# A hybrid diffusion trunk layer on Trainium2: setting the order of the DMA queue in the second phase of the first feed-forward block

## The chip, the cores and the metric

The kernel runs on one core of a Trainium2 chip, in one launch. The time of a kernel is the device time of the launch in microseconds, as the median of its runs. The engines of the core are named as the profile names them: PE is TensorE (matmuls), PEld its weight loads, DVE is VectorE, ACT is ScalarE, POOL is GpSimd, and SP is SyncE, which here only issues DMA transfers.

## The reference

One layer of a transformer-like trunk is computed on 1024 latent tokens and 256 context tokens, all of width 1024, in float32:

```python
# m_l, m_c: nine modulation vectors each, from silu(c) @ ada_w + ada_b (latent) and c_ctx (context)
x   = x   + 0.5 * m_l[2] * swiglu(modulate(rms_norm(x,   norm1_w), m_l[0], m_l[1]), ffn1_w1, ffn1_w3, ffn1_w2)
ctx = ctx + 0.5 * m_c[2] * swiglu(modulate(rms_norm(ctx, norm1_w), m_c[0], m_c[1]), ffn1_w1, ffn1_w3, ffn1_w2)
y   = token_mixing(modulate(rms_norm(x, norm2_w), ...), modulate(rms_norm(ctx, norm2_w), ...), ...)
x   = x + m_l[5] * y
x   = x + 0.5 * m_l[8] * swiglu(modulate(rms_norm(x, norm3_w), ...), ffn2_w1, ffn2_w3, ffn2_w2)
return rms_norm(x, final_norm_w)

def swiglu(h, w1, w3, w2):
    return (silu(h @ w1) * (h @ w3)) @ w2
```

The hidden width of the feed-forward blocks (FFN1 and FFN2) is 2816. The change lies in FFN1, in the product with w2 for the latent tokens and in what is done beside it.

## The kernel before

**Precision.** TensorE multiplies in a reduced float32 format. So each operand is split into a high part and a low part (`split`: ScalarE writes the high part, L59; VectorE, for some tiles GpSimd, subtracts it to get the low part, L60), and each product is three matmuls (`mm3`: high x high at L64, high x low at L65, low x high at L66).

**Order.** A scheduler at build time puts the instructions of each engine into a fixed list, which the engine then works off in order, waiting at each instruction for what it needs. It goes through time by its own estimate of durations and takes for each engine the ready instruction of the best priority; a tile is ready to be written when its room is free. The priority is the place in the program; inside `high_priority(offset=n)` it is n places earlier, with a negative n later (`low(n)` gives n places later). Inside `manual_schedule(engines=...)` the instructions of these engines keep the order in which the program lists them.

**FFN1, first phase** (`hidden`, `chain`). The 22 slices of the hidden width are taken in pairs. The latent tokens are two halves of 512 (tg 0 and 1). Of a pair of slices and the two halves, a 2 x 2 block product, seven products are formed instead of eight, from sums of tiles. The inputs of these sums, T1 to T4, stand ready as split tiles. T4 has the room `hh10`, `hl10` to `hh13`, `hl13` (the first half of the room of `self.h[1]`), and is read by the last of the seven products of each chain (`prod(w4, t4, a, False)`). `g_out` writes seven combinations of the gated results of each pair to device memory (`gd[1..7, p]`, p = 0 to 10), and `w2_sums` two combinations of the weights w2 (`sd[0..1, p]`).

**FFN1, second phase** (`back6`, then `prod(4, ...)` later). The product with w2 is formed the same way, six of its seven products in `back6`, in the order 1, 2, 6, 5, 7, 3. Each product has 11 steps (p), and a step is 12 matmuls: one tile of g, one of the weights, four output blocks, `mm3` each. In each step `pair` loads g's raw tile (`raw_half(self.gd[i, p])`, L260), splits it into one of four rooms `h{h,l}00` to `h{h,l}03`, loads the weight tile (`w2_tile`) and splits it into one of six rooms `whi`, `wlo`, all 150 places ahead (`WPRI`). Raw tiles of g and of the weights share six rooms named `raw` (`NR`). For products 7 and 3 the weight is a difference of two loaded tiles, which have eight rooms of their own, `h{h,l}04` to `h{h,l}07` (`raw2`, L368; L392 subtracts).

**Beside the second phase** `feed` runs one entry of `plan` per step. It loads the context tokens (`load_x`, eight tiles of 128 KB, L777) at steps 0 to 7, and the sixteen tiles of x (L1465), which were given up during the first phase, at steps 8, 10, ... 38; and it makes the first norm of the context (`ctx1`, in steps 22, 24, 27 and 30 to 37). All of these are placed by the scheduler like all else, as early as it finds room. After products 2, 7 and 3 the results are added to x (`add4`, L442); later x is written to device memory (`spill`, L1507).

**After it** comes the context's own FFN1 (`classic` and `Y`, pairs of slices). Beside it the second half (tg 1) of the latent tokens gets its second norm: `norm2(1, 0)` sums the squares (L173, L176, L177) ahead of the loop, and one further entry of `pend` is listed behind each pair: entry 1 forms the column sums on TensorE (`rstd_col`, L186) and the root (L1049, L1050), entry 2 spreads it over the rows (`rstd_rows`, L193, L202, and L1477), entries 3 to 10 write one normed tile each into the room of `self.h[1]` (`norm_k`, L216, L217, L222). Then follow `prod(4)`, the context's projections, the mixing stage, FFN2 and the final norm.

Of the kernel before, what the change touches and what calls it, by code (L numbers as in the profile page):

```python
# [2 lines left out]

# [7 lines left out]
F32 = mybir.dt.float32  # L11
# [5 lines left out]
P = 128  # L17
D = 1024
KD = D // P
DFF = 2816  # L20
NF = DFF // P
NP = NF // 2
# [8 lines left out]
class Trunk:  # L31
# [50 lines left out]
    def cond(self):  # L82
        self.cs = [self.cond_row("c")]
        self.junk = self.tile(self.dp, [P, D], mybir.dt.bfloat16, "junk")
        self.ada, self.ab = -1, tuple(range(AB))

# [308 lines left out]
    def hidden(self, f0, mods=lambda: None):  # L395
# [8 lines left out]
        for p in [*range(f0 // 2 - 1), NP - 1]:  # L404
            self.w2_sums(p)

    def pair(self, i, p):
        slots = [f"0{k}" for k in range(4)]
        t = self.hslot(slots[self.nslot % 4])
        self.nslot += 1  # L410
        with self.tc.high_priority(offset=WPRI):
            self.split(self.raw_half(self.gd[i, p]), *t)
            return self.half(self.w2_tile(i, p)), t

    def hslot(self, s):
        return tuple(self.tile(self.hp, [P, 512], F32R, f"h{c}{s}") for c in "hl")
# [107 lines left out]
    def ffn_open(self, i, gates, pool):  # L524
        self.w1, self.w3, self.w2 = (self.I[f"w{i}{j}"] for j in (1, 3, 2))
        self.gates_m, self.fp, self.s, self.g = gates, pool, {}, {}
        self.gd, self.sd = self.gds[i - 1], self.sds[i - 1]
        self.nraw, self.nslot, self.feed = -1, 0, iter(())

    def stile(self):  # L530
        return self.tile(self.fp, [P, 512], F32, "s", self.ns)
# [119 lines left out]
    def first1(self, pools, n1):  # L651
# [52 lines left out]
        for st in range(KD):  # L704
# [6 lines left out]
            if st + 1 < KD:  # L711
                self.mod_col(9 + st, (0,), True)
                if st >= SH:
                    self.mod_col(st + 1, (0,), True)
# [684 lines left out]
    def run(self):  # L1399
        nc, tc, I = self.nc, self.tc, self.I  # L1400
        S = {}

        def opn(name, side="left"):
            S[name] = tc.tile_pool(name=name, bufs=1, reuse_waits="tile", side=side)
            return S[name].__enter__()
# [34 lines left out]
        self.ada, self.ab = -1, (2, 3, 4, 0)  # L1440
        todo = [(8 * m + k, ctxs) for m, ctxs in EMODS for k in range(KD) if m or not 1 <= k <= SH]
        todo.reverse()
# [11 lines left out]
        hc = opn("hc", "right")  # L1454
# [4 lines left out]

        plan = defaultdict(list)  # L1460
        for k in range(KD):
            plan[k].append(lambda k=k: self.load_x((None, None, hc), (2,), (k,)))
        for i, (tg, k) in enumerate((tg, 4 * q + k) for tg, q in ((0, 0), (1, 1), (0, 1), (1, 0)) for k in range(4)):
            o = TGS[tg][0]
            plan[8 + 2 * i].append(lambda tg=tg, k=k, o=o: nc.sync.dma_start(self.x[tg][k], I["xT"][k * P:(k + 1) * P, o:o + 512]))  # L1465
        nrm = {}

        def norm_step(tg, i, a, b):
            n = TGS[tg][1]
            if i == 0:  # L1470
                nrm[tg] = self.squares(self.x[tg], n, n2)
            elif i == 1:
                nrm[tg] = self.rstd_col(nrm[tg], n, n2)
            elif i == 2:
                pr = self.rstd_rows(nrm[tg], n, n2)
                nrm[tg] = self.scr(n2, "nrb")[:, :n]
                nc.scalar.copy(nrm[tg], pr)  # L1477
            else:
                self.norm_k(tg, i - 3, a, b, nrm[tg], n2)

        ctx1 = lambda i: norm_step(2, i, self.mcol(1, 1), self.mcol(0, 1))
        norm2 = lambda tg, i: norm_step(tg, i, self.mcol(4, int(tg == 2)), self.mcol(3, int(tg == 2)))
        for i, at in enumerate((22, 24, 27, *range(30, 30 + KD))):
            plan[at].append(lambda i=i: ctx1(i))

        CT = [(2, 0, 256)]
# [12 lines left out]

        self.feed = feed()  # L1500
        self.psN = self.psB
        self.back6(False)

        def spill(tg):
            o = TGS[tg][0]
# [32 lines left out]
        for tg in LATTG:  # L1538
            o, n = TGS[tg]
# [39 lines left out]

NT2 = 5  # L1580
AB = 5
SH = 2
NR = 6
EMODS = ((5, (0,)), (2, (0, 1)), (1, (1,)), (0, (1,)), (4, (0, 1)), (3, (0, 1)), (7, (0,)), (6, (0,)))
# [39 lines left out]
def layout(inputs):  # L1624
# [7 lines left out]
    A["adaT"] = c(g["ada_w"][0].T).reshape(72, P, D)  # L1632
    A["adaN"] = c(g["ada_w"][0][:, P:(SH + 1) * P].reshape(KD, P, SH, P).transpose(2, 1, 0, 3)).reshape(SH, P, D)
    A["ccol"] = c(np.stack([g["c"].reshape(KD, P), g["c_ctx"].reshape(KD, P)]).transpose(2, 1, 0)).reshape(P, 2 * KD)
# [65 lines left out]
```

## Time and profile before

| | |
|---|---|
| median of 3 runs | 2186.89 us (2180.45 to 2189.05) |
| the profiled execution | 2184.39 us, its span 2182.6 us |
| busy PE, DVE, ACT, POOL | 97%, 70%, 45%, 13% of the span |
| mean granted TensorE clock | 0.993 |
| DMA | 373.39 MB, mean 171 GB/s; 51.9% of 16 engines' span |
| FFN1's second phase (six products) | from 467.3 to 657.5 us |
| the context's FFN1 | from 657.5 us on |

A row of the timeline has the start and the duration in us, the engine, the line of the kernel, the operation with the tiles that it writes and reads, and in brackets the idle time of the engine before it and what ended that. A row of the windows has for each engine the busy time in us and (x) the instructions in that stretch, then the granted clock of TensorE, the mean busy share of the 16 DMA engines and what they moved in GB/s. A matmul that reaches over the edge of a window counts in both. A row of the DMA issues has the number of transfers, the size of one and the median time in us from issue to landing.

### The profile page before, as it was taken

To read this page: it belongs to the slowest core of one execution; us is meant where nothing else is said; L and a number is where in the kernel's file an instruction comes from. 1 tells how busy PE (TensorE), PEld (TensorE's weight loads), DVE (VectorE), ACT (ScalarE), POOL (GpSimd) and SP (SyncE) were. 2 spreads that over 40 slices of the span, in tenths; PEclk is the share of its full clock that TensorE was granted. 3 is DMA by queue.
4 is the path that set the end of the run, shared out by engine and by line. 5 is a ranking of instruction groups with operands and counts; after the bars stand their busy time and mean duration, and the time that the engine had idled before them with its cause. 6 is when DMAs were issued, how large, how long until landed. Compare 5 with 4: busy or idle time off the path is not lost. (4 is left out here: it accounts for less than half of the span.)

```text
span 2182.6 us, 32925 instructions
## 1 busy us (share of the span) xinstructions
PE 2123.4 (97%) x11558; PEld 1807.1 (83%) x11558; DVE 1530.7 (70%) x2735; ACT 981.2 (45%) x1811; POOL 278.1 (13%) x285
## 2 busy tenths in 40 slices
PE   8999999999999999999989999999999999999998
PEld 7888888887789999987777987788878888888888
DVE  7889999755678556744665546758777667664686
ACT  4434334344545545546454335525343433434553
POOL 0000000000016553611132112200000000000000
PEclk8999999999999999999999999999999999999999
DMA  9267768478775566553312322324134444467674
GB/s 330 83 231 245 268 220 276 158 234 278 246 254 179 172 188 197 177 155 104 92 58 70 94 59 90 120 81 166 63 120 158 147 159 159 150 208 249 218 241 145
DMA packets 202934, 373.39 MB, mean 171 GB/s; under 512 B 24016, under 2 KB 37264, under 8 KB 202768
## 3 DMA queue, kind: packets, MB, share of 16 engines
q1 hardware_dynamic: 202336, 371.16, 51.9%
q8 instruction: 90, 1.47, 0.3%
q14 instruction: 76, 0.62, 0.1%
q10 hardware_dynamic: 432, 0.13, 0.0%
HBM read 296.72 MB, written 66.09 MB: 166 GB/s over the span
## 5 line engine op out<-in xcount | busy, mean ns | idle before, releaser
L59 ACT ACTIVATE whi<-raw 128x512 fp32r<-128x512 f32 (+1 forms) x647 | 398.9, 623 | 711.4 <-issue 210.2
L60 DVE TENSOR_TENSOR wlo<-raw,whi 128x512 fp32r<-128x512 f32 (+1 forms) x533 | 368.5, 694 | 307.1 <-ACT whi L59 301.5
L64 PE MATMUL psa<-hh,whi 128*128 128x512 f32 (+1 forms) x1444 | 531.4, 368 | 1.7 <-ACT hh L59 0.7
L65 PE MATMUL psa<-hl,whi 128*128 128x512 f32 (+1 forms) x1444 | 530.9, 368 | 1.0 <-DVE hl L60 1.0
L66 PE MATMUL psa<-hh,wlo 128*128 128x512 f32 (+1 forms) x1444 | 530.0, 367 | 0.0
L64 PEld LDWEIGHTS psa<-hh,whi 128*128 128x128 f32 x1444 | 273.9, 190 | 45.5 <-ACT hh L59 1.4
L65 PEld LDWEIGHTS psa<-hl,whi 128*128 128x128 f32 x1444 | 273.9, 190 | 43.8 <-DVE hl L60 2.5
L66 PEld LDWEIGHTS psa<-hh,wlo 128*128 128x128 f32 x1444 | 273.9, 190 | 41.5
L64 PE MATMUL psb<-hh,whi 128*128 128x512 f32 (+1 forms) x680 | 260.4, 383 | 2.2 <-ACT hh L59 1.7
L65 PE MATMUL psb<-hl,whi 128*128 128x512 f32 (+1 forms) x680 | 260.6, 383 | 1.6 <-DVE hl L60 1.4
L66 PE MATMUL psb<-hh,wlo 128*128 128x512 f32 (+1 forms) x680 | 259.8, 382 | 0.6 <-DVE wlo L60 0.6
L60 POOL TENSOR_TENSOR wlo<-raw,whi 128x512 fp32r<-128x512 f32 (+1 forms) x114 | 153.0, 1361 | 194.3 <-ACT whi L59 188.3
L65 PEld LDWEIGHTS psb<-hl,whi 128*128 128x128 f32 x680 | 127.8, 188 | 29.0 <-DVE hl L60 4.4
L64 PEld LDWEIGHTS psb<-hh,whi 128*128 128x128 f32 x680 | 127.9, 188 | 28.7 <-ACT hh L59 2.8
L66 PEld LDWEIGHTS psb<-hh,wlo 128*128 128x128 f32 x680 | 127.8, 188 | 25.5 <-DVE wlo L60 1.0
L1050 POOL TENSOR_TENSOR nr<-nr,mhalf 128x4 f32<-128x4 f32 (+1 forms) x11 | 11.6, 1057 | 867.7 <-ACT hh L59 482.5
L60 DVE TENSOR_TENSOR hl<-raw,hh 128x512 fp32r<-128x512 f32 x159 | 112.2, 711 | 13.2 <-ACT hh L59 12.2
L59 ACT ACTIVATE hh<-raw 128x512 fp32r<-128x512 f32 x159 | 97.6, 619 | 16.5 <-DMA raw<-gd 14.8
L64 PE MATMUL psa<-whi,hh 128*128 128x256 f32 (+1 forms) x320 | 93.1, 291 | 1.4 <-ACT s L1004 1.2
L65 PE MATMUL psa<-wlo,hh 128*128 128x256 f32 (+1 forms) x320 | 93.4, 292 | 1.0 <-DVE wlo L60 0.9
L66 PE MATMUL psa<-whi,hl 128*128 128x256 f32 (+1 forms) x320 | 92.5, 289 | 0.0
L126 DVE CUSTOM_DVE_ANT_0 junk<-ada,condc,cols 128x1024 bf16<-128x1024 f32 x62 | 79.3, 1279 | 5.4 <-DMA ada<-in_adaT 5.1
(397 smaller groups left out, 3723.2 us busy)
## 6 DMA issues: line engine op xcount, KB each, us to landing
raw<-in_w SPq DMA_DIRECT2D x374, 256.0 KB, 3.0
gd<-s SPq DMA_DIRECT2D x154, 256.0 KB, 2.7
raw<-gd SPq DMA_DIRECT2D x154, 256.0 KB, 3.7
ada<-in_adaT SPq DMA_DIRECT2D x76, 512.0 KB, 4.8
s<-in_w SPq DMA_DIRECT2D x66, 256.0 KB, 4.7
sd<-s SPq DMA_DIRECT2D x44, 256.0 KB, 2.8
hh<-in_w SPq DMA_DIRECT2D x44, 256.0 KB, 3.9
raw<-sd SPq DMA_DIRECT2D x44, 256.0 KB, 3.0
```

The costliest lines, as they stand in the source:

```text
L59: nc.scalar.activation(hi, src, AF.Copy)
L60: (eng or nc.vector).tensor_tensor(out=lo, in0=src, in1=hi.bitcast(F32), op=ALU.subtract)
L64: mm(ps, wa[0], xa[0], start=start, stop=False, skip_group_check=more)
L65: mm(ps, wa[0], xa[1], start=False, stop=False, skip_group_check=more)
L66: mm(ps, wa[1], xa[0], start=False, stop=stop, skip_group_check=more)
L126: nc.vector.tensor_tensor_reduce(out=self.junk, in0=t, in1=self.cs[s], scale=1.0, scalar=self.col("ada_b")[:, j:j + 1], op0=ALU.mult, op1= ...
L1050: nc.gpsimd.tensor_tensor(out=r, in0=r, in1=self.mhalf[:, :n], op=ALU.pow)
```

## The change

Four things are changed, all in the order of work; the arithmetic and the transfers are the same.

1. The loads of g and of the weights in `back6` are no longer issued in the step that uses them, 150 places ahead. `loaded` keeps a list, and lists in each step the loads of the step five later (`AHEAD`), at the priority of its place; the first step lists the loads of the first six. `back6` runs inside `manual_schedule` for SP, so that all the loads listed there, those of `feed` too, keep that order among themselves.
2. The raw tiles of g get rooms of their own: `raw_g` goes round the sixteen rooms `hh10`, `hl10`, `hh11`, ... `hl17` of `self.h[1]`. The six `raw` rooms are left to the weights.
3. The loads in `plan` are spaced otherwise: the context's eight tiles in steps 12, 13, 15, 16, 18, 19, 21 and 22, the tiles of x in the steps of `xat`. The context's norm comes in steps 24, 27, 30 and 33 to 40.
4. Of the second half's norm, entries 1 to 10 are listed 150 places later (`NLOW`).

```diff
@@ -1,4 +1,4 @@
-from collections import defaultdict
+from collections import defaultdict, deque
 from contextlib import ExitStack, nullcontext
 
 import numpy as np
@@ -404,13 +404,32 @@
         for p in [*range(f0 // 2 - 1), NP - 1]:
             self.w2_sums(p)
 
+    def raw_g(self, src):
+        self.ng += 1
+        t = self.tile(self.hp, [P, 512], F32, f"h{'hl'[self.ng % 2]}1{self.ng // 2 % 8}")
+        self.nc.sync.dma_start(t, src)
+        return t
+
+    def loaded(self, i, p):
+        if not self.steps:
+            return self.raw_half(self.gd[i, p]), self.w2_tile(i, p)
+        while len(self.ahead) <= min(AHEAD, self.nsteps):
+            j, q = next(self.steps)
+            self.ahead.append((self.raw_g(self.gd[j, q]), self.w2_tile(j, q)))
+        self.nsteps -= 1
+        return self.ahead.popleft()
+
     def pair(self, i, p):
         slots = [f"0{k}" for k in range(4)]
         t = self.hslot(slots[self.nslot % 4])
         self.nslot += 1
+        if self.steps:
+            g, w = self.loaded(i, p)
         with self.tc.high_priority(offset=WPRI):
-            self.split(self.raw_half(self.gd[i, p]), *t)
-            return self.half(self.w2_tile(i, p)), t
+            if not self.steps:
+                g, w = self.loaded(i, p)
+            self.split(g, *t)
+            return self.half(w), t
 
     def hslot(self, s):
         return tuple(self.tile(self.hp, [P, 512], F32R, f"h{c}{s}") for c in "hl")
@@ -525,7 +544,7 @@
         self.w1, self.w3, self.w2 = (self.I[f"w{i}{j}"] for j in (1, 3, 2))
         self.gates_m, self.fp, self.s, self.g = gates, pool, {}, {}
         self.gd, self.sd = self.gds[i - 1], self.sds[i - 1]
-        self.nraw, self.nslot, self.feed = -1, 0, iter(())
+        self.nraw, self.nslot, self.feed, self.steps = -1, 0, iter(()), None
 
     def stile(self):
         return self.tile(self.fp, [P, 512], F32, "s", self.ns)
@@ -1459,13 +1478,18 @@
 
         plan = defaultdict(list)
         for k in range(KD):
-            plan[k].append(lambda k=k: self.load_x((None, None, hc), (2,), (k,)))
-        for i, (tg, k) in enumerate((tg, 4 * q + k) for tg, q in ((0, 0), (1, 1), (0, 1), (1, 0)) for k in range(4)):
+            plan[12 + k + k // 2].append(lambda k=k: self.load_x((None, None, hc), (2,), (k,)))
+        xat = (1, 4, 7, 10, 24, 26, 28, 30, 32, 34, 36, 38, 39, 40, 42, 43)
+        for at, (tg, k) in zip(xat, ((tg, 4 * q + k) for tg, q in ((0, 0), (1, 1), (0, 1), (1, 0)) for k in range(4))):
             o = TGS[tg][0]
-            plan[8 + 2 * i].append(lambda tg=tg, k=k, o=o: nc.sync.dma_start(self.x[tg][k], I["xT"][k * P:(k + 1) * P, o:o + 512]))
+            plan[at].append(lambda tg=tg, k=k, o=o: nc.sync.dma_start(self.x[tg][k], I["xT"][k * P:(k + 1) * P, o:o + 512]))
         nrm = {}
 
         def norm_step(tg, i, a, b):
+            with self.low(NLOW if tg == 1 and i else None):
+                norm_part(tg, i, a, b)
+
+        def norm_part(tg, i, a, b):
             n = TGS[tg][1]
             if i == 0:
                 nrm[tg] = self.squares(self.x[tg], n, n2)
@@ -1480,7 +1504,7 @@
 
         ctx1 = lambda i: norm_step(2, i, self.mcol(1, 1), self.mcol(0, 1))
         norm2 = lambda tg, i: norm_step(tg, i, self.mcol(4, int(tg == 2)), self.mcol(3, int(tg == 2)))
-        for i, at in enumerate((22, 24, 27, *range(30, 30 + KD))):
+        for i, at in enumerate((24, 27, 30, *range(33, 33 + KD))):
             plan[at].append(lambda i=i: ctx1(i))
 
         CT = [(2, 0, 256)]
@@ -1499,7 +1523,11 @@
 
         self.feed = feed()
         self.psN = self.psB
-        self.back6(False)
+        self.ng, self.ahead, self.nsteps = -1, deque(), 6 * NP - 1
+        self.steps = ((i, p) for i in (1, 2, 6, 5, 7, 3) for p in range(NP))
+        with tc.manual_schedule(engines={mybir.EngineType.SP}):
+            self.back6(False)
+        self.steps = None
 
         def spill(tg):
             o = TGS[tg][0]
@@ -1579,6 +1607,8 @@
 
 NT2 = 5
 AB = 5
+AHEAD = 5
+NLOW = 150
 SH = 2
 NR = 6
 EMODS = ((5, (0,)), (2, (0, 1)), (1, (1,)), (0, (1,)), (4, (0, 1)), (3, (0, 1)), (7, (0,)), (6, (0,)))
```

## The prediction

> **What bounds the kernel now.** I read the page first, then the windows of FFN1's second phase, then the TensorE timeline at its holes, then the DMA views around them.
>
> ```profile
> span 2182.6 us, 32925 instructions
> ## 1 busy us (share of the span) xinstructions
> PE 2123.4 (97%) x11558; PEld 1807.1 (83%) x11558; DVE 1530.7 (70%) x2735; ACT 981.2 (45%) x1811; POOL 278.1 (13%) x285
> ```
>
> TensorE is the bound over the whole span, so only a hole in its stream can be won. The profiled execution took 2184.39 us for this span of 2182.6; the median of the runs, 2186.89, lies 2.5 us above it. The change touches the stretch from 467 to about 720 us. The second phase is six products of eleven steps. One product per row:
>
> ```profile
> core 0: us, PE busy (x) PEld busy (x) DVE busy (x) ACT busy (x) POOL busy (x), PEclk, DMA share, GB/s
> 467.30:497.20 29.90, 29.90 (x134) 24.75 (x133) 18.60 (x32) 10.79 (x20) 0.00 (x0) 1.00 0.88 292
> 497.20:530.90 33.70, 31.30 (x133) 24.52 (x132) 16.35 (x27) 15.66 (x29) 0.00 (x0) 1.00 0.83 266
> 530.90:566.00 35.10, 32.79 (x142) 25.13 (x140) 23.93 (x43) 14.27 (x27) 1.00 (x1) 1.00 0.89 297
> 566.00:597.70 31.70, 31.02 (x134) 24.64 (x134) 20.16 (x36) 19.97 (x39) 0.00 (x0) 1.00 0.68 211
> 597.70:627.60 29.90, 29.90 (x134) 24.75 (x133) 20.75 (x34) 13.17 (x25) 0.00 (x0) 1.00 0.89 297
> 627.60:657.50 29.90, 29.90 (x134) 24.76 (x133) 24.59 (x37) 11.07 (x19) 7.04 (x5) 1.00 0.67 213
> ```
>
> The reader sees that an undisturbed product takes 29.90 us, so a step is 29.90 / 11 = 2.72 us, and that the second to fourth products take 33.70 + 35.10 + 31.70 - 3 x 29.90 = 10.8 us too much. The context norm's eight small matmuls lie in the third; such a group of eight takes 671.92 - 671.01 = 0.9 us (rows further down). **9.9 us of holes** are left. What they wait for:
>
> ```profile
> 522.69 0.39 PE L66 MATMUL psb<-hh,wlo 128*128 128x512 f32 x1
> 524.75 0.50 PE L64 MATMUL psb<-hh,whi 128*128 128x512 f32 x1 [1.68 <-ACT hh L59]
> 525.56 0.50 PE L65 MATMUL psb<-hl,whi 128*128 128x512 f32 x1 [0.30 <-DVE hl L60]
> ```
>
> The split on ScalarE is named, but ScalarE is busy under half of that product; it waits for the tile itself. Meanwhile the queue is full of other transfers:
>
> ```profile
> GB/s 205 275 273 259 303 295 265 325 350 366 169 270 184 271 365 273 129 297 222 284 378 337 222 279 274 249 330 277 305 178 280 285 331 273 357 355 280 270 274 375
> x<-in_xT SPq DMA_DIRECT2D x16, 256.0 KB, 4.7
> hl<-in_w SPq DMA_DIRECT2D x7, 256.0 KB, 4.6
> xd<-x SPq DMA_DIRECT2D x4, 256.0 KB, 5.1
> hh<-in_w SPq DMA_DIRECT2D x2, 256.0 KB, 5.0
> ```
>
> That is the DMA view from 497 to 566 us. All sixteen x tiles and nine weight tiles for products 7 and 3, which start at 566 + 31.7 us, go out here, between the tiles that the next step needs. Only six raw rooms, shared by g and w, give those a lead of three steps.
>
> **The change part by part.** It adds and removes no transfer and no arithmetic: the same 66 g tiles, 66 weight steps, sixteen x and eight context tiles, and the same splits. What moves is order.
>
> *x and context spaced, queue in order.* Four x tiles go out with the first ten steps, eight half-size context tiles with steps 12 to 22, twelve x tiles with steps 24 to 43; the nine early weight tiles go back to their turn. That is 12 + 9 = 21 tiles fewer before step 24, and g and w no longer share six rooms: the rule "next step's tiles first" now holds. Steps 15 to 43 then carry at most 2 + 12/20 = 2.6 tiles per 2.72 us, which even the slowest rate below serves. Each transfer costs its SyncE issue as before. So the 9.9 us go, if nothing takes their place.
>
> *g's raw tiles in h's room.* Something does. Steps 0 to 7 put g into the room of T4, and T4 is what the last product of phase one reads:
>
> ```profile
> 464.54 0.39 PE L64 MATMUL psb<-hh,whi 128*128 128x512 f32 x1
> 464.99 0.39 PE L66 MATMUL psb<-hh,wlo 128*128 128x512 f32 x1
> ...
> 467.26 0.39 PE L64 MATMUL psa<-hh,whi 128*128 128x512 f32 x1
> ```
>
> The first pair of T4 is read until 464.99 + 0.39 = 465.4; g's first tile can't be issued earlier, and as it heads a fixed order, every weight, x and later g tile of the phase is queued behind it on SyncE. Before, these went out from 445 us on:
>
> ```profile
> raw<-gd SPq DMA_DIRECT2D x6, 256.0 KB, 4.6
> raw<-in_w SPq DMA_DIRECT2D x5, 256.0 KB, 4.9
> ```
>
> (DMA view, 440 to 465 us.) These eleven tiles of lead are lost. How long a tile takes to land, and what else the queue has to carry at that time (raw tiles from 440 to 470 us; the window and the issues from 465 to 505 us):
>
> ```profile
> DMA to landing us min/median/max: 2.6/4.2/5.7
> 465.00:505.00 40.00, 40.00 (x178) 33.14 (x177) 25.05 (x42) 16.74 (x34) 0.00 (x0) 1.00 0.85 279
> gd<-s SPq DMA_DIRECT2D x6, 256.0 KB, 3.6
> s<-in_w SPq DMA_DIRECT2D x6, 256.0 KB, 4.7
> sd<-s SPq DMA_DIRECT2D x4, 256.0 KB, 3.7
> ```
>
> First step: g lands at 465.4 + 2.6 = 468.0, w one tile later, its split takes 0.62 (row L59 of the page's groups, shown below). TensorE starts at about 468.0 + 0.85 + 0.62 = 469.5 instead of 467.26: **2.2 us**, or 3.8 with the median landing.
>
> ```profile
> L59 ACT ACTIVATE hh<-raw 128x512 fp32r<-128x512 f32 x159 | 97.6, 619 | 16.5 <-DMA raw<-gd 14.8
> ```
>
> Then the queue must catch up. Step 14, the last before the extra traffic is over, needs 30 tiles for steps 0 to 14, 6 stores of g, 10 transfers of the weight sums and 3 x tiles: 49. With t us per tile it is ready at 465.4 + 2.6 + 48t + 0.62 and wanted at 467.26 + 14 x 2.72 = 505.3. The delay by then, which includes the start, is S = 48t - 36.7, and at least 2.2. The tile time t isn't in the trace for a queue that is never short of requests. Bounds: 0.262 MB at the window's 279 GB/s is 0.94; with its idle share taken out, 0.94 x 0.85 = 0.80. The new queue has up to six weight and sixteen g tiles asked for, so it lies nearer to the second; I take 0.85. S = 4.1 us, with 2.2 to 8.4 for the range. I add 0.8 for short waits of a step whose parts land just in time, like the 0.30 above. **Second phase: 9.9 - 4.1 - 0.8 = 5.0 us gained.**
>
> *Clock.* A gap of over 2 us can cost more than itself. In the context's FFN1, after the phase:
>
> ```profile
> 711.56 0.28 PE L66 MATMUL psb<-ghi,wlo 128*128 128x256 f32 x1
> 713.92 0.38 PE L64 MATMUL psb<-ghi,whi 128*128 128x256 f32 x1 [2.08 <-ACT ghi L59]
> 714.87 0.56 PE L65 MATMUL psb<-glo,whi 128*128 128x256 f32 x1 [0.57 <-DVE glo L60]
> 715.00:718.40 3.40, 3.40 (x16) 3.40 (x17) 3.00 (x4) 0.90 (x2) 2.64 (x2) 0.51 0.53 162
> ```
>
> After two waits close together the granted clock is 0.51 for 3.4 us, which costs 1.7 us; after the gap at 522.69 it stayed 1.00. The start gap of 2.2 us lies between these two cases, so I charge half, **0.8 us lost**. [...]
>
> *Second half's norm at lower priority.* Its column sum on TensorE now stands right behind the first pair of the context's FFN1 and waits for VectorE's nacc:
>
> ```profile
> 671.01 1.05 PE L186 MATMUL psb<-ones,nacc 128*128 128x1 f32 x8 [1.85 <-DVE nacc L177]
> 671.92 0.36 PE L64 MATMUL psa<-hh,whi 128*128 128x256 f32 x1
> 711.30:721.70 10.40, 7.75 (x50) 7.35 (x49) 9.21 (x16) 4.92 (x10) 5.52 (x4) 0.84 0.51 155
> 674.90:680.70 5.80, 5.80 (x50) 5.76 (x49) 5.34 (x9) 2.24 (x5) 4.79 (x4) 1.00 0.42 135
> ```
>
> By the last row 48 matmuls take 5.80 us; a pair of slices has 144, so 17.4 us, and lists some 70 other instructions. 150 places of 214 are about 12 us, by when nacc is long done: **1.9 us gained**. Nobody misses it: the half's normed tiles are first read in the mixing stage. The making of these tiles is another matter. It makes VectorE late at 711 us, where 48 matmuls take 10.40 us: 4.6 us lost, the slow clock among them. They are listed one per pair, behind pairs 3 to 10, and yet run during the first three, in room that the scheduler thought free; a step of 150 doesn't forbid that. They come later and meet other work. Between nothing and 4.6 no row decides; I take half, **2.3 us gained**. The context norm comes two to three steps later and ends at step 40 of 66; it is first used after the phase: nothing.
>
> Sum: 5.0 - 0.8 + 1.9 + 2.3 = 8.4 us. 2184.39 - 8.4 = 2176.0 for a profiled execution; 2.5 more for the median: **2178.5 us**.
>
> **The rivals.** All but the norm's part hangs on t.
>
> *The queue keeps up (t at 0.80 or below).* S is the start alone: 9.9 - 2.2 - 0.8 = 6.9, no clock drop, and the norm's tiles meet nothing: 6.9 + 1.9 + 4.6 = 13.4, so 2173.5. For it: stretches of over 330 GB/s in the view above. Against: nothing here holds them for ten microseconds.
>
> *The hole moves to the front (t about 0.92).* S = 7.5. The last two products take three tiles a step and lose their nine early ones: from step 44 on there are 66 tiles, 4 of x, 4 spills and 6 weights of the context's FFN1 that find the raw rooms free, 80 in all, against 22 x 2.72 = 59.8 us and a lead of three steps (four rooms for the splits of g), 8.2: 80 x 0.92 - 68.0 = 5.6 late. 9.9 - 7.5 - 5.6 + 1.9 = -1.3, so 2188: no change.
>
> *The queue falls behind at both ends (t of 1.0 or more): slower.* The same two terms. The mean over the phase supports it:
>
> ```profile
> DMA packets 26997, 48.92 MB, mean 257 GB/s; under 512 B 2995, under 2 KB 3379, under 8 KB 26983
> ```
>
> (480 to 670 us.) 0.262 MB at 257 GB/s is 1.02. S = 12.3, the end is 80 x 1.02 - 68.0 = 13.6 late, together 25.9 against 9.9 before and 1.9 won: 14.1 slower, 2201. At t = 1.0 it is 11.5; from there it counts as slower. Against it: this mean holds stretches with nothing asked for. For it: a fixed order can hold the queue idle too, as one transfer that waits for its room stops all behind it. [...] That is a rule against a fixed order; the start here shows its price, the 2.2 us, and the trace shows no more of it.
>
> *The lower priority does nothing.* Then 1.9 and 2.3 are missing: 2182.7, inside the forecast's range.
>
> **How the numbers follow.** 0.5%, 10.9 us, is about what a measurement of this kernel can tell from no change. Forecast with its own range of 2175 to 2184: 0.46, a quarter of it beyond 10.9 us. Queue keeps up: 0.27, faster. Hole moves: 0.13, the same. Slower: 0.14. Faster 0.27 + 0.11 = 0.38, same 0.35 + 0.13 = 0.48, slower 0.14. The range goes down to 2170, where all that the sum names is won (9.9 + 1.9 + 4.6 = 16.4), and up to 2193, where t is about 0.96; beyond lie some 0.05 and 0.10.
>
> **What would show it.** Right: g's first load issued at 465 us, a TensorE gap of 2 to 4 us at 467; small holes until about 505, none from 510 to 657; x tiles one to three steps apart; the column sum some 10 us later, without wait; the first product at 32 to 34 us, the next five near 29.9. Wrong: first product still at 29.9 (T4's room doesn't bind); holes after 585 (the end binds); DVE waits in the context's FFN1 as long as before; or changes of several microseconds after 900 us, where the change writes nothing but a new order could come out of the scheduler.

## The result and the profile after

The change made the kernel slower. The median of five runs each went from 2186.89 us (2180.45 to 2189.05) to 2199.86 us (2196.58 to 2201.57); the ratio is 1.0059, with a 95% interval of 1.0039 to 1.0078. The profiled execution took 2196.58 us, its span 2194.8, which is 12.2 us more than before. The forecast was 2178.5.

The windows of the second phase after, one product per row behind the row of the gap ahead of the first:

```profile
core 0: us, PE busy (x) PEld busy (x) DVE busy (x) ACT busy (x) POOL busy (x), PEclk, DMA share, GB/s
467.60:470.10 2.50, 0.37 (x2) 0.00 (x1) 2.50 (x5) 1.26 (x2) 0.00 (x0) 0.97 0.97 365
470.10:514.80 44.70, 34.40 (x132) 27.73 (x133) 22.10 (x34) 18.02 (x31) 0.00 (x0) 0.81 1.00 351
514.80:544.80 30.00, 30.00 (x134) 24.82 (x133) 17.70 (x31) 15.74 (x33) 0.00 (x0) 1.00 0.73 231
544.80:575.60 30.80, 30.80 (x142) 25.63 (x141) 21.33 (x39) 15.27 (x29) 0.70 (x1) 1.00 0.81 265
...
635.40:665.30 29.90, 29.90 (x133) 24.76 (x132) 24.15 (x36) 11.21 (x19) 7.03 (x5) 1.00 0.48 160
```

The holes of before are gone: the five later products run without a wait (the 30.80 holds the context norm's eight small matmuls). All of the phase's loss stands in the first two rows. The first product takes 44.7 us instead of 29.9, with a gap of some 2.3 us ahead of it: 17.1 us lost, where before lost 9.9. TensorE's timeline and the windows behind its two waits, after (these windows have TensorE's busy time alone):

```profile
470.10 0.80 PE L64 MATMUL psa<-hh,whi 128*128 128x512 f32 x1 [2.13 <-ACT whi L59]
484.92 0.79 PE L64 MATMUL psa<-hh,whi 128*128 128x512 f32 x1 [10.30 <-ACT whi L59]
```

```profile
470.00:473.40 3.40, 3.30 (x8) 0.51 0.94 328
484.90:490.20 5.30, 5.28 (x12) 0.50 1.01 375
490.00:500.00 10.00, 10.00 (x44) 0.98 1.06 390
```

Two waits, 2.1 and 10.3 us, both for a weight's high part, and half clock behind each for 3.4 and 5.3 us. Half of 8.7 us is 4.35, and 2.3 + 10.3 + 4.35 = 17.0 is the 17.1 but for 0.1. What held the weight is in the timeline of SyncE, after, where each row is the issue of a transfer, and in VectorE's rows of the same time:

```profile
465.96 0.32 SPq L410 DMA_DIRECT2D hh<-gd  x1
466.37 0.39 SPq L260 DMA_DIRECT2D raw<-in_w  x1
467.46 3.45 SPq L349 DMA_DIRECT2D gd<-s  x5
470.96 2.86 SPq L379 DMA_DIRECT2D s<-in_w  x6
475.69 0.33 SPq L381 DMA_DIRECT2D sd<-s  x1
477.05 0.33 SPq L383 DMA_DIRECT2D sd<-s  x1
477.43 0.42 SPq L410 DMA_DIRECT2D hl<-gd  x1
478.84 0.32 SPq L381 DMA_DIRECT2D sd<-s  x1
479.57 0.32 SPq L383 DMA_DIRECT2D sd<-s  x1
479.94 0.44 SPq L260 DMA_DIRECT2D raw<-in_w  x1
```

```profile
474.96 0.69 DVE L380 TENSOR_TENSOR s<-s,s 128x512 f32<-128x512 f32 x1 [3.80 <-DMA s<-in_w]
476.33 0.69 DVE L382 TENSOR_TENSOR s<-s,s 128x512 f32<-128x512 f32 x1 [0.68 <-DMA s<-in_w]
478.12 0.69 DVE L380 TENSOR_TENSOR s<-s,s 128x512 f32<-128x512 f32 x1 [1.10 <-DMA s<-in_w]
478.85 0.69 DVE L382 TENSOR_TENSOR s<-s,s 128x512 f32<-128x512 f32 x1
```

Step 0's two loads go out at 466. Step 1's weight goes out at 479.94, 13.6 us later. Between them stand g's last five stores, six loads for the last two weight sums and the four stores of these sums. Each of the four stores is issued just when VectorE's sum ends (474.96 + 0.69 = 475.65, and 475.69), and the sums wait for their loads. So the list, which SyncE works off in order, holds step 1's weight behind a chain of load, sum and store whose results no step loads until some 50 us later, five steps ahead of the third product.

The rest of the loss lies in the context's FFN1. TensorE's waits from 665.4 to 760 us, after (in total, how many, the longest):

```profile
PE psa L66 <- POOL wlo L60: 2.9, 6, 0.8
PE psb L64 <- ACT ghi L59: 2.4, 1, 2.4
PE psa L64 <- ACT whi L59: 1.8, 1, 1.8
PE psb L65 <- DVE glo L60: 1.0, 1, 1.0
PE psb L64 <- DVE x L574: 0.8, 2, 0.4
```

and the same of the kernel before, from 657 to 750 us:

```profile
PE psb L64 <- ACT ghi L59: 2.1, 1, 2.1
PE psb L186 <- DVE nacc L177: 1.8, 1, 1.8
PE psb L65 <- DVE glo L60: 0.6, 1, 0.6
```

The column sum's wait is gone, the stall behind ScalarE's ghi is still there, and six waits for GpSimd's wlo are new. Counted at the same matmuls, after is 7.9 us late at the end of the phase and 13.8 us late at the end of this stretch: 6 us lost here. Of the 13.8, 1.6 us net come back later (last section).

### The profile page after: what moved, and what is told of

Its sections match the earlier page's. It is cut to its first block, busy times and chain, and to the rows that moved or that the text cites. A ratio compares the mean times of both kernels' runs of the same rounds, so it can differ in the third digit from the quotient of the medians.

```text
span 2194.8 us, 32881 instructions
## 1 busy us (share of the span) xinstructions
PE 2123.0 (97%) x11558; PEld 1808.8 (82%) x11558; DVE 1531.0 (70%) x2735; ACT 982.0 (45%) x1811; POOL 277.6 (13%) x285
## 5 line engine op out<-in xcount | busy, mean ns | idle before, releaser
L60 DVE TENSOR_TENSOR hl<-raw,hh 128x512 fp32r<-128x512 f32 x93 | 65.2, 708 | 9.0 <-ACT hh L59 8.8
L64 PEld LDWEIGHTS psa<-whi,hh 128*128 128x128 f32 x320 | 61.7, 193 | 2.7 <-ACT s L1023 1.4
```

The lines of the kernel that those rows point to most:

```text
L60: (eng or nc.vector).tensor_tensor(out=lo, in0=src, in1=hi.bitcast(F32), op=ALU.subtract)
L64: mm(ps, wa[0], xa[0], start=start, stop=False, skip_group_check=more)
```

## The experiments

Each has a ratio to the kernel before, run on the same chip, with its 95% interval.

| run | median us | ratio | interval |
|---|---|---|---|
| e1_ahead_again | 2188.08 | 1.0002 | 0.9993 to 1.0012 |
| e2_other_rooms | 2199.02 | 1.0050 | 1.0032 to 1.0068 |
| e3_norm_in_place | 2193.96 | 1.0035 | 1.0022 to 1.0048 |
| e4_norm_alone | 2193.57 | 1.0023 | 1.0013 to 1.0032 |
| e5_sums_later | 2191.87 | 1.0033 | 1.0022 to 1.0044 |
| e6_ahead_norm_in_place | 2183.91 | 0.9991 | 0.9981 to 1.0000 |
| e7_ahead_other_rooms | 2183.87 | 0.9994 | 0.9985 to 1.0003 |
| e8_norm_40_lower | 2181.84 | 0.9986 | 0.9975 to 0.9997 |
| e9_all_four | 2178.06 | 0.9961 | 0.9946 to 0.9976 |
| e10_order_alone | 2176.99 | 0.9957 | 0.9943 to 0.9971 |
| e11_norm_alone_vector | 2178.30 | 0.9963 | 0.9949 to 0.9977 |
| e12_best_vector | 2168.43 | 0.9918 | 0.9904 to 0.9932 |
| e13_vector_alone | 2174.77 | 0.9952 | 0.9933 to 0.9971 |

One thing limits what single profiled executions say of the second phase. e4, e11 and e13 leave its lists on TensorE and SyncE as they are in before, and yet it took 186.7, 191.6 and 189.0 us there, against 190.3 in before. A difference of 3 or 4 us in the phase is not shown by one execution.

**e1, the loads 150 places ahead again.** The changed kernel with

```diff
-        if self.steps:
-            g, w = self.loaded(i, p)
         with self.tc.high_priority(offset=WPRI):
-            if not self.steps:
-                g, w = self.loaded(i, p)
+            g, w = self.loaded(i, p)
```

> The loads of the second phase are listed 150 places ahead again (as before the change); all else as changed. Theory of the list: the 10.7 us gap in the first product comes from SyncE's list alone, in which five stores of g and ten transfers of the weight sums, two of them waiting for VectorE, stand ahead of step 1's tiles because these lost their 150 places. Then the first product falls from 44.7 us to 31 to 34 us, and the kernel from 13 us over before to 0 to 3 us over it. Theory of the rate (the prediction's): the same transfers must go through the same engines, so the gap is only cut up; the first product stays above 40 us and the kernel 8 us or more over before.

The window of the first product in e1:

```profile
471.10:504.00 32.90, 32.22 (x133) 25.90 (x134) 18.61 (x30) 15.00 (x26) 0.00 (x0) 0.95 0.99 356
```

The first product takes 32.9 us instead of 44.7, with the same transfers at the same rate (356 and 351 GB/s): the place in the list was the cause, not the rate. The phase gains 4.1 us on before (e4's unchanged phase 3.7). The context's FFN1 loses 7.5 us, and 3.0 come back at the places of the last section, so the time is that of before.

**e2, other rooms.** The changed kernel, g's raw tiles starting at hh14 instead of hh10:

```diff
-        self.ng, self.ahead, self.nsteps = -1, deque(), 6 * NP - 1
+        self.ng, self.ahead, self.nsteps = 7, deque(), 6 * NP - 1
```

> g's first eight raw tiles go into the rooms of the second half's tiles 4 to 7, which are read by the last product but one of the first phase, instead of T4's rooms, which are read by the last; priorities as changed. Theory of the rooms (the prediction's): the first gap of 2.5 us goes, and with it the lead of 2.7 us is won for all later tiles. Theory of the list: the first gap goes, three steps instead of one get into SyncE's list ahead of the weight sums, and the long gap of 10.7 us comes three steps later and is 2 to 5 us long: the first product takes 33 to 37 us, the kernel is 3 to 6 us over before. If only the rooms count, the long gap keeps some 8 us or more and the kernel is 9 us or more over before.

The short gap at the start went, since T4's room was its cause. The long one did not shrink as I expected: it moved a few steps on and took 9.9 us, and the first product 43.1. These are the numbers that I expected if only the rooms count; that it is the list all the same, the SyncE timeline shows:

```profile
479.66 0.33 SPq L381 DMA_DIRECT2D sd<-s  x1
...
483.75 0.32 SPq L383 DMA_DIRECT2D sd<-s  x1
484.16 0.44 SPq L260 DMA_DIRECT2D raw<-in_w  x1
```

It is the same chain: the first tiles overtake it, and the next weight, at 484.16, stands behind it. A tile that comes earlier only changes which step finds the chain in its way.

**e3, the norm in place.** The changed kernel with `NLOW = None`.

> The second half's norm has its old priority; all else as changed. Theory of the norm: the 5.9 us that the context's FFN1 loses come from the lower priority alone, which puts a third projection ahead of the first Y, so that GpSimd's splits set the pace. Then the kernel comes to 6 to 8 us over before, and TensorE's waits for GpSimd's wlo go. Rival: the loss comes from the weights of the context's FFN1, whose first loads go out 16 us later than before; then it stays, and the kernel stays 12 to 14 us over before.

**e4, the norm alone.** The kernel before with the fourth part of the change alone (`norm_part`, `NLOW = 150`).

> The kernel before with the lower priority of the second half's norm alone. Theory of the norm: 3 to 6 us slower than before, with TensorE waiting for GpSimd's wlo behind three projections in a row. Rival (late weights): no loss; the 1.9 us of the column sum are won, so 0 to 4 us faster than before.

Both came out as the theory of the norm had it. With the norm in place the waits for GpSimd are gone and before's three are back. The norm alone costs 0.23%. In the profiled executions the context's FFN1 takes 7.5 us longer, with the very waits of after, among them the six for wlo, 2.9 us in all.

TensorE's lists differ: before has 120 projection matmuls ahead of the first Y block, after and e4 have 185. The scheduler, with the norm out of the way, had put 65 more projection matmuls there, and their weights are the ones that GpSimd splits.

**e5, the weight sums later.** The changed kernel with the last two sums listed inside the phase, behind its steps 2 and 4; the loads without priority, as changed:

```diff
         for p in [*range(f0 // 2 - 1), NP - 1]:
-            self.w2_sums(p)
+            if f0 == 2:
+                self.w2_sums(p)
...
+        for p, at in ((0, 2), (NP - 1, 4)):
+            plan[at].append(lambda p=p: self.w2_sums(p))
```

> The changed kernel with one thing else: the last two weight sums (ten transfers and four sums on VectorE) are written inside the second phase, behind its steps 2 and 4, and not ahead of it; the loads keep the priority of the change. Theory of the list (what stands ahead of a tile in SyncE's list, not the rate of transfer, made the start late): g's five stores still stand between step 0's and step 1's tiles, the six loads and the two stores that wait for VectorE don't; the gap of 10.7 us goes, the first one of 2.3 us stays; first product 32 to 35 us, against 44.7, and the time 7 to 10 us below the changed kernel: 2190 to 2193 us, ratio to before 1.001 to 1.003. Rival, the rate (the transfers wanted in the first steps are too many for the queue, in whatever order): the sums' transfers still fall into the first product, which stays over 40 us, and the time stays within 3 us of 2199.

The ratio is 1.0033, after's 1.0059: some 6 us better (the medians differ by 8.0, but come from different chips). The gap of 10.3 us is gone, but the first product takes 38.4 us, where 32 to 35 were forecast. Three waits of 8.3 us in all are left: 2.2 ahead of the first step, 2.9 ahead of the second, behind g's five stores alone, and 3.3 at 508 us, near the end of the product. The last is made by the sums at their new place, as SyncE's rows show:

```profile
494.92 1.36 SPq L379 DMA_DIRECT2D s<-in_w  x3
501.73 0.33 SPq L381 DMA_DIRECT2D sd<-s  x1
502.64 0.33 SPq L383 DMA_DIRECT2D sd<-s  x1
503.53 0.40 SPq L260 DMA_DIRECT2D raw<-in_w  x1
```

SyncE waits over 5 us for a sum, and the next weight goes out behind it. So of the 10.3 us some 7 came from the sums and the rest from g's stores, and steps 2 and 4 were too early a place for the sums.

**e6 and e7, both losses undone.** e6 is e1 with `NLOW = None`; e7 is e6 with e2's rooms.

> Both parts of the loss undone: the loads inside the lines of 150 places' priority as before the change, and the norm's part of the second half at its old priority; what is left of the change is the five steps ahead, the rooms and the spaced loads. Theory (two causes that add): the first run with the loads ahead gained 4.1 us in the phase and lost 4.9 in the context's FFN1; without that loss the time is 3 to 6 us under the kernel before, 2181 to 2184.5 us, ratio 0.997 to 0.9985. Rival (the losses share a cause, so that the second is not the norm's): within 1.5 us of before.

> As the run before this one in the list, and g's first tiles take the rooms hh14 to hl17, which are free earlier than hh10 to hl13. Theory: the gap of 3.0 us at the start of the phase goes too, with the half clock behind it (0.7 us or so): 3 to 4 us more, 2178 to 2181 us, ratio 0.995 to 0.997; first product 30 to 31 us. Rival (the start then waits for the weights or for g's own stores instead): under 1 us gained by the rooms.

Both missed. e6 gained 0.1%, at the edge of its interval, where 0.15 to 0.3% was expected, and the rooms added nothing. In e6's profiled execution the phase did gain 3.6 us; it loses 1.4 of it soon after, to a lower clock (0.68 from 667.7 to 671.1 us, 0.81 from 671.1 to 674.5) behind a wait that before has as well (last section). In e7 the gap at the start is gone, and one of 4.1 us stands from 487.8 on; the first product takes 35.9 us, not 30 to 31. Its SyncE timeline:

```profile
472.15 6.34 SPq L349 DMA_DIRECT2D gd<-s  x6
478.54 2.81 SPq L379 DMA_DIRECT2D s<-in_w  x6
...
484.89 0.33 SPq L383 DMA_DIRECT2D sd<-s  x1
...
485.76 0.45 SPq L410 DMA_DIRECT2D hl<-gd  x1
```

With 150 places the loads of the first seven steps pass the sums; step 7's tile (485.76) does not. The chain from after is still there, and the wait has moved seven steps on.

**e8, the norm 40 places lower.** e7 with `NLOW = 40`, so that Y stands again behind 120 projection matmuls and the column sum inside Y.

> As the run before this one, and the norm's part of the second half at a priority lower by 40 places, not by 150. In the list of TensorE the column sum then stands behind the context FFN1's first fourteen matmuls of the first Y block, which itself stands behind 120 projection matmuls as before the change (150 places: behind 185). Theory of the order (150 places cost because they put a third and fourth projection ahead of Y, so that GpSimd's splits set the pace): the loss of 5 us doesn't appear, the column sum's wait of 2.1 us is gone, and the time is 0 to 3 us under the run before. Rival (any lowering costs, as the norm's tiles then meet ScalarE's splits later): 3 to 6 us over the run before, with waits for the context's high parts from ScalarE.

2.0 us under e7 in the median; the intervals overlap, so that the gain of itself is not shown (in the profiled executions both are 1.3 us ahead of before at 745 us, and the 2 us come far behind the change). But the loss of 5 us did not come, and neither did a wait for wlo. With GpSimd's splits, then, the lower priority costs time by the order that it brings, not by itself.

**e9, all four, and e10, the order alone.** e9 is e8 with e5's sums, at steps 14 and 18; e10 is the same without the 150 places.

> The run with the norm 40 places lower (loads ahead again, other rooms), and the last two weight sums written inside the phase, behind its steps 14 and 18. In the runs before this one the wait at the start of the phase came back three to seven steps later, as one wait of 4.5 to 4.7 us with half clock behind it: the sums' six loads and two of their stores stand in SyncE's list ahead of step 7's tile. Theory of the list: with the sums out of the way step 7's tile is issued at 479 us or so instead of 486, the wait of 4.7 us goes and the half clock with it; the first product takes 30 to 32 us (37.5 in that run), the time is 5 to 7 us under it: 2175 to 2178 us, ratio to before 0.995 to 0.9965. Rival, the rate (g's five to seven stores and the tiles of seven steps are too much for the queue, whatever else stands in it): the wait stays, 3 us or more, and less than 2 us is gained.

> As the run above, but the loads keep the change's own priority (none), so that g's last stores stand between the first four steps' tiles in SyncE's list. Theory of the list: a store of g waits for VectorE's product or for a difference (0.7 us each) and holds the tile behind it; with the sums gone what is left is 0 to 3 us in the first four steps: 2176 to 2181 us. Rival (the 150 places are needed by themselves): the first product stays over 36 us, time 2183 or more.

Both times are as the theory of the list had it. The first product of e9 and, beside it, the SyncE rows that answer to those of e7:

```profile
467.50:498.10 30.60, 30.60 (x133) 24.50 (x132) 20.87 (x33) 17.83 (x30) 0.00 (x0) 1.00 0.98 353
```

```profile
472.40 6.33 SPq L349 DMA_DIRECT2D gd<-s  x6
...
479.26 0.44 SPq L411 DMA_DIRECT2D hl<-gd  x1
```

Step 7's tile goes out at 479.26 instead of 485.76, and no wait is left in the phase: 30.66 us for the first product, then 29.92 each. g's six stores are still there and cost nothing. Nor does the chain at its new place: SyncE issues a sum's loads at 500.29 and waits until 508.85 for the sum, but by then it is five steps ahead, and no step waits.

e10 has one wait of 1.9 us, and behind it a granted clock of 0.54 from 474 to 476 us and 0.61 from 476 to 478: a store of g at 464.74 stands ahead of the second step's tiles, which go out 1.4 us later than in e9 (465.12 and 463.73). Its phase takes 184.9 us, e9's 181.3, and at 745 us it is 4.0 us behind e9. It comes to the same time, as e9 loses some at two places far behind the change (1118 and 1153 us) and e10 does not: at the first e9's granted clock is 0.59 from 1118 to 1121 us and 0.88 from 1121 to 1125, and e10's mean from 1070 to 1220 us is 1.00. So that the 150 places are not needed with the chain gone is not shown.

**e11 and e13, the splits on VectorE.** e11 is e4, and e13 the kernel before, each with

```diff
-            self.classic(f, (2,), ..., eng=[nc.gpsimd if e else None for e in CENG])
+            self.classic(f, (2,), ..., eng=[nc.vector if e else None for e in CENG])
```

> The kernel before, with only the norm's part of the second half at the lower priority by 150 places (that alone cost 5 us), and the context FFN1's low parts of w1 and w3 on VectorE instead of GpSimd (0.69 us for 1.29). In TensorE's list Y then stands again behind 122 projection matmuls, not 185. Theory (the order of Y with GpSimd's slower splits made the loss): no waits for the low part of a weight, and at most 2 us over the kernel before. Rival (the norm's tiles, late, meet the splits on ScalarE and VectorE, whatever GpSimd does): 4 to 7 us over the kernel before.

> The kernel before with one thing else: the context FFN1's low parts of w1 and w3 on VectorE instead of GpSimd, the norm at its old priority. Theory that the lowered norm was right in itself and lost by GpSimd's pace: the column sum's wait of 2.1 us and the stall of 2.35 and 0.95 us stay here, so that this gains under 2 us: 2184 to 2187 us, ratio 0.999 to 1.001. Rival, that GpSimd held the context's FFN1 back in the kernel before as well and the norm's priority adds nothing: 2177 to 2180 us, as the run with both.

e11 gained 0.37%: no loss, as the theory had it, but a gain that neither side had. Y stands behind 122 projection matmuls in it, so the long list without GpSimd's splits was not run. e13 shows where the gain comes from, and here the rival won: the kernel before gains 0.48% by VectorE's splits alone, with the norm at its old priority. e11 and e13 don't differ beyond their intervals, so the lower priority adds nothing that these runs can show. In e13 TensorE does not wait in the whole stretch from 657 to 745 us:

```profile
657.00:745.00 88.00, 88.00 (x733) 87.72 (x732) 77.87 (x148) 51.95 (x97) 1.01 (x1) 1.00 0.58 188
```

(before has 83.31 of 88.00 there). Even the column sum's wait is gone, at the same place in TensorE's list. VectorE's group of the first instruction of each normed tile in that stretch (instructions, busy us, mean ns of one), before and then e13:

```profile
L216 DVE SCALAR_TENSOR_TENSOR nt<-x,modl,nrb 128x512 f32<-128x512 f32 x8 | 10.0, 1262 | 1.6 <-ACT nrb L1477 1.5
```

```profile
L216 DVE SCALAR_TENSOR_TENSOR nt<-x,modl,nrb 128x512 f32<-128x512 f32 x8 | 5.8, 745 | 0.0
```

The same instruction takes 1262 ns in the mean among GpSimd's subtractions and 745 without them (L177, which adds up the column sum's input: 1057 and 684). The trace of before shows the same within itself:

```profile
708.02 0.73 DVE L216 SCALAR_TENSOR_TENSOR nt<-x,modl,nrb 128x512 f32<-128x512 f32 x1
714.74 1.76 DVE L216 SCALAR_TENSOR_TENSOR nt<-x,modl,nrb 128x512 f32<-128x512 f32 x1
```

```profile
714.47 3.18 POOL L60 TENSOR_TENSOR wlo<-raw,whi 128x512 fp32r<-128x512 f32 x2 [7.25 <-ACT whi L59]
```

GpSimd is idle for 7.25 us up to 714.47; the two of the eight L216 that fall into that time take 0.73 and 0.74 us, the other six 1.0 to 1.8. So the norm's tiles did not by themselves make VectorE late at 711 us; at the 1.0 to 1.8 us that they take beside GpSimd's subtractions, they did. (e13 gives VectorE another list as well, so that the slower instructions are the whole cause is not shown.) Why VectorE's instructions take longer there, no run shows.

Not all of e13's gain is this. Of the 13.4 us between the profiled executions 7.3 are won from 657 to 745 us and 1.5 more by 900; 2.8 come at two places far behind the change, those of before's low clock in the last section (0.68 from 1126.7 to 1130.1 us; 0.85 and 0.59 from 1160 to 1166 us); over the whole execution e13's mean granted clock is 0.995, before's 0.993.

**e12, all that helped.** e9 with `NLOW = 150` and VectorE's splits.

> All that helped together: loads ahead again, g's first tiles in the later rooms, the last two weight sums inside the phase, the norm's part of the second half 150 places lower, and the context FFN1's low parts of w1 and w3 on VectorE. Theory (two independent places that add): the second phase as in the run with all four, 181 us from its first product to the context's FFN1, and the context's FFN1 without waits, which was worth 5 to 6 us in the run with the norm alone: 2171 to 2174 us, ratio to before 0.993 to 0.9945. Rival (VectorE, busier, splits g's and the context's tiles later and gives the gain back): no faster than the 2178 us of the run with all four.

2168.43 us, 0.82% under the kernel before and below the forecast. The two places add: at the same matmuls it is 9.1 us ahead of before late in the phase and 15.4 us ahead after the context's FFN1. It beats both kernels.

## Why the prediction was wrong

Of the 20.6 us between the forecast and the profiled execution some 11.5 lie in the second phase (4.2 us gained in the forecast, the clock's 0.8 taken off, and 7.3 lost) and 10 in the norm's part.

**"Queue in order ... the rule 'next step's tiles first' now holds": this step failed.** The diff takes the loads out of `high_priority(offset=WPRI)`, and I read that as no more than an order among themselves. It also gave up the 150 places that had carried them past g's last stores and the weight sums. I did count these sixteen transfers in the queue, but as a share of its rate (48t), not as entries in SyncE's list that stand ahead of step 1 and wait for VectorE. e5 (against after) and e9 (against e8) show it by moving the sums alone: the gap of 10.3 us went, 2.9 of it stayed behind g's stores, and in e9 none. The last rival named the mechanism ("one transfer that waits for its room stops all behind it") and then dismissed it: "the trace shows no more of it". The trace of before had these stores in it; their place in the new list was to be worked out from the program.

**The tile time of 0.85 us: mis-sized.** With enough asked for, the queue moved 390 GB/s over ten microseconds (after, 490 to 500 us), so 0.262 MB take 0.67 us. By S = 48t - 36.7 nothing but the start would then be lost. e9's first product of 30.66 us agrees, though ten of the 49 transfers come later there. The two rivals on the slower side needed a t of 0.92 and more, which the queue did not have; the one with 0.80 or below had the rate right. The rates from which I took t, 257 and 279 GB/s, stand beside a busy share of the DMA engines of 0.79 and 0.85, the 390 beside 1.06: by my reading, those of a queue that had too little asked for.

**The start gap: right.** Forecast 2.2 to 3.8 us from T4's room; 2.3 in after, 2.7 in e1, none with other rooms.

**The holes of 9.9 us gone, none from 510 to 657: right.** Products 2 to 6 run at 29.92 us. But 9.9 was the size of one execution: e4, e13 and e11, with the same lists there, had 6.2, 8.6 and 11.1.

**The clock: 0.8 charged, 4.35 lost,** 1.7 of it behind the 2.1 us gap (granted clock 0.51), where the rival of a queue that keeps up had "no clock drop", and 2.65 behind the 10.3 us gap that I had not forecast (0.50).

**The norm: 4.2 us gained in the forecast, 6 lost.** The column sum did run later and without its wait (1.9, right). The second half of the sum failed: I asked only what the norm's tiles would meet, not what the scheduler would put into their place, and I blamed the stall at 711 us on the tiles alone. A wait for ghi of 2.4 us stood in e4 with the tiles later, and none was left in e13 with the tiles at their old priority.

## What to carry to other kernels

When a load loses its priority or its order is fixed, list what then stands ahead of it in the issuing queue, and look there for stores that wait for an engine: here two sums with their loads and stores cost some 7 us, though the queue moved 351 GB/s over that product. Moving a few tiles past the chain only passed the wait to the next one; listing the chain where the loads already have a lead of five steps took it away. And where VectorE is late beside a busy GpSimd, compare the duration of the same instruction with and without GpSimd (here 1262 and 745 ns) before blaming the order.

## What the runs showed that I had not expected

**A gap of the same length lowered the clock in one run and not in another.** Behind the column sum's wait (1.85 us in before, 1.86 in e6) the granted clock stayed at 1.00 in before and fell to 0.68 in e6:

```profile
671.00:674.40 3.40, 3.39 (x28) 1.00 0.63 196
```

```profile
667.70:671.10 3.40, 3.34 (x20) 0.68 0.64 196
```

Far behind the change, before and after have the same wait (2.45 and 2.48 us), and there it is before that pays, in the first of these rows, and after that does not:

```profile
1126.70:1130.10 3.40, 3.40 (x18) 0.68 0.27 62
```

```profile
1140.70:1144.10 3.40, 3.40 (x23) 1.00 0.24 59
```

That gave 1.5 us of the loss back, and a second such place 1.6 (before 0.85 and 0.59 from 1160 to 1166 us, after 1.00 from 1172 to 1178); some 1.5 us were lost again, as behind one more wait that both have (2.32 us) after has a granted clock of 0.59 and 0.56, from 1398 to 1402 us, and before has 1.00 (1384 to 1394 us). In the rows above the waits of 1.86 and 2.45 us had the lower clock behind them and those of 1.85 and 2.48 us had not; so the length alone does not decide it, and what does is not shown. My estimate from the 1.5, 1.6 and 1.5 us: here a change that shifts the work behind it by a few microseconds could move the time by one to three, up or down, without any merit of its own. e10, with a mean of 1.00 from 1070 to 1220 us where before has 0.98, had some of it, and so, by the time won at the same places, had e13.
